# Two small DMAs through DRAM in place of a diagonal product: spreading the token factors of the norms in a two-layer hybrid decoder trunk

## The chip, the cores and the metric

The kernel runs on one core of one Trainium2 chip. The metric is the device time of one execution in microseconds (us); lower is better. Engines are named as in the profile: PE (TensorE matmul) and PEld (its weight loads), DVE (VectorE), ACT (ScalarE), POOL (GpSimd) and SP (SyncE, which here only issues DMAs). A time such as "at 298.30" counts from the first instruction of the profiled execution.

## The reference, cut to what matters

```python
def rmsnorm(x, g):
    y = x * rsqrt(mean(x * x, axis=-1) + EPS)        # one factor r per token
    return y * g                                     # one gain per channel

for l in range(2):                                   # x is (256 tokens, 1024)
    h = rmsnorm(x, norm1[l])
    hq, hf, hi, hg, aq, ak, av, ga, gb = split_cols(h @ w_in[l])
    ...                                              # gated recurrence, windowed attention
    x = x + mix @ w_o[l]
    h2 = rmsnorm(x, norm2[l])
    x = x + (silu(h2 @ w_gate[l]) * (h2 @ w_up[l])) @ w_down[l]
return rmsnorm(x, final_norm)
```

All is float32. The norm's factor r belongs to a token, so it may be left out of the matmul's input and multiplied into its result.

## The kernel before, in words

Every weight comes from DRAM as a 1 MB tile `raw` (SP's queue), and is split into a high part `wh` (ACT, a cast) and a low part `wl` (DVE, `raw - wh`); three matmuls of the parts make one product of nearly full precision. Five `wh` and `wl` tiles rotate. The 256 tokens are two blocks `t` of 128.

A `Norm` object holds what one norm needs. `turn` transposes x on PE, multiplies by the gain and splits it into `xx`, the input of the matmuls, *without* the token factor. `square`, `partial` and `scale` sum the squares; the last step is a power on POOL, which leaves the factor of each token in `r[t]`, a column of 128 partitions by 1.

Where a product has the tokens on its partitions (`form_a`: attention's inputs, values, gates), the factor is `r[t]` itself, the scale operand of the instruction that empties PSUM. Where it has the tokens along the row (`form_b`: the recurrence's f and q, called `pb` in the trace, and the FFN's gate `pg` and up `pu`), each partition needs the factors of all 256 tokens. `spread` (L321) makes that tile, `rb`, 128 partitions by 256. Before the change it takes, for each t, a DVE multiply of the identity by `r[t]` (tile `dg`, one buffer) and a float32 matmul of an all-ones matrix with `dg` into the PSUM tile `rp` (tag "at", two buffers, shared with attention); then an ACT copy takes `rp` to `rb` (one buffer). The profile counts each of these matmuls as two, since float32 goes through PE in two passes.

`spread` is called four times, once for each of the two norms in each layer:

- norm1 (`n1`): at L715, ahead of the second half of the values `v`. The first reader of `rb` is the multiply of f at L726, behind two `pb` blocks.
- norm2 (`n2`): at L835, within the first `gate_up` (L817), as soon as the first gate block is out of PSUM. The first reader is `mid` (L824): DVE multiplies `zg` by `rb`, ACT takes the sigmoid, DVE multiplies the two. Up blocks `pu` are emptied (`join`, L259) behind that.

Work is issued engine by engine in one order that a scheduler sets from the order of the code: every engine runs its own list from the front, so an instruction that waits holds all behind it. In `gate_up` DVE's list has, behind the multiply by `rb`, the splits `wl` of the next weights and the joins that give PSUM buffers back to PE. There are four PSUM buffers for matmul blocks (tag "mm"); a `gate_up` uses all four (two `pg`, two `pu`), so the next `gate_up`'s first `pu` needs the join of this one's first `pu`. Recorded lines of compute instructions are all L55, the helper that records them, so the trace is read by tiles.

Of the kernel before, what the change touches and what calls it, by code (L numbers as in the profile page):

```python
# [7 lines left out]
F32 = mybir.dt.float32  # L8
# [4 lines left out]
ALU = mybir.AluOpType  # L13
AX = mybir.AxisListType

P = 128
D = 1024
S = 256
NT = S // P
# [21 lines left out]
def trunk(ctx, tc, x, norm1, w_in, lb_logits, hg_norm, attn_sinks, w_pa, w_pb, w_o, norm2,  # L41
          w_gate, w_up, w_down, final_norm, const_f, out):
    nc = tc.nc
    pinned, pe_order = [False], [False]

    class Ordered:
        def __init__(self, engine):
            self.engine = engine
            self.always = engine is nc.tensor
# [10 lines left out]
    V, A, G, T = (Ordered(e) for e in (nc.vector, nc.scalar, nc.gpsimd, nc.tensor))  # L60
# [7 lines left out]
    wp = ctx.enter_context(tc.tile_pool(name="wp", bufs=NW))  # L68
    big = ctx.enter_context(tc.tile_pool(name="big", bufs=6))
    sm = ctx.enter_context(tc.tile_pool(name="sm", bufs=2))  # L70
    pp = ctx.enter_context(tc.tile_pool(name="pp", bufs=2, space=bass.MemoryType.PSUM))

    def psum(name, tag="mm"):
        return pp.tile([P, 512], F32, tag=tag, name=name, bufs=4 if tag == "mm" else 2)
# [13 lines left out]
    ones = cp.tile([P, P], F32, tag="ones", name="ones")  # L88
    G.memset(ones, 1.0)
    ident = cp.tile([P, P], F32, tag="ident", name="ident")  # L90
# [185 lines left out]
    class Norm:  # L276
        def __init__(self, gain, name):
            self.gain, self.name = gain, name
            self.xx = hp.tile([P, KT, 2, S], F32R, tag="xx", name=f"xx_{name}")
            self.xh, self.xl = self.xx[:, :, 0, :], self.xx[:, :, 1, :]  # L280
            self.rb = sm.tile([P, 1, S], F32, tag="rb", name=f"rb_{name}", bufs=1)
            self.ss = sm.tile([P, NT, 3], F32, tag="ss", name=f"ss_{name}")
            self.r = [sm.tile([P, 1], F32, tag=f"r{t}", name=f"r_{name}{t}") for t in range(NT)]

# [34 lines left out]
            yield 1  # L319

        def spread(self):  # L321
            rp = psum(f"rp_{self.name}", "at")
            for t in range(NT):
                dg = sm.tile([P, P], F32, tag="dg", name=f"dg_{self.name}{t}", bufs=1)
                tc.keep_in_program_order(V.tensor_scalar(dg, ident, self.r[t], None, ALU.mult))
                T.matmul(rp[:, t * P:(t + 1) * P], ones, dg, start=True, stop=True)
            A.copy(self.rb[:, 0, :], rp[:, :S])

        def wide(self):
            return self.rb.to_broadcast([P, 2, S])  # L330
# [32 lines left out]
    def layer(l, n1):  # L363
# [349 lines left out]
        for c in range(2):  # L713
            if c == 1:
                spread()  # L715
            yield from proj(f"v{c}", lambda t, ps: evac_scaled(v[t][:, c * 512:(c + 1) * 512], ps, rs[t]))
# [293 lines left out]
```

## Time and profile before

| | us |
|---|---|
| median of three runs | 951.02 (951.01 to 951.48) |
| the profiled execution | 951.18 |
| its span, first to last instruction | 949.5 |
| PE busy | 934.3 |
| DVE busy | 678.5 |
| ACT busy | 538.4 |
| POOL busy | 16.5 |

The mean granted clock of PE is 0.998. DMA moves 161.11 MB in 110930 packets, 170 GB/s on average, nearly all of it the weights on SP's queue; ACT issues a few small loads at the start and half of the output. POOL issues no DMA. The time outside the span (951.18 less 949.5) is 1.7 us.

How to read the rows of the timeline: start, duration, engine, line, operation, tiles as out<-in, sizes, how many were merged into the row, and in brackets how long the engine was idle ahead of it and what ended that. Matmuls overlap in the pipe, so the distance from one start to the next is what a matmul costs PE, not its duration.

### The profile page before, as it was taken

To read this page: it belongs to the slowest core of one execution; us is meant where nothing else is said; L and a number is where in the kernel's file an instruction comes from. 1 tells how busy PE (TensorE), PEld (TensorE's weight loads), DVE (VectorE), ACT (ScalarE), POOL (GpSimd) and SP (SyncE) were. 2 spreads that over 40 slices of the span, in tenths; PEclk is the share of its full clock that TensorE was granted. 3 is DMA by queue.
4 is the path that set the end of the run, shared out by engine and by line. 5 is a ranking of instruction groups with operands and counts; after the bars stand their busy time and mean duration, and the time that the engine had idled before them with its cause. 6 is when DMAs were issued, how large, how long until landed. Compare 5 with 4: busy or idle time off the path is not lost.

```text
span 949.5 us, 14350 instructions
## 1 busy us (share of the span) xinstructions
PE 934.3 (98%) x5706; PEld 778.0 (82%) x5706; DVE 678.5 (71%) x1176; ACT 538.4 (57%) x914; POOL 16.5 (2%) x28
## 2 busy tenths in 40 slices
PE   7999999999999999999999999999999999999996
PEld 5878887888888888888878888878788888888885
DVE  6567879976677766766575677898857777667664
ACT  6556596545446545554465776955454565455542
POOL 1000000000000000000000000000000000000000
PEclk9999999999999999999999999999999999999999
DMA  7645454544455566556466444554445566556541
GB/s 282 225 128 175 143 167 137 168 143 159 154 176 177 180 193 203 179 181 198 153 203 197 133 134 133 177 179 134 151 154 185 160 203 191 177 181 202 193 134 44
DMA packets 110930, 161.11 MB, mean 170 GB/s; under 512 B 2768, under 2 KB 64400, under 8 KB 110864
## 3 DMA queue, kind: packets, MB, share of 16 engines
q1 hardware_dynamic: 110160, 159.12, 51.6%
q10 hardware_dynamic: 704, 1.10, 0.3%
q8 instruction: 44, 0.72, 0.3%
q14 instruction: 22, 0.18, 0.1%
HBM read 159.15 MB, written 1.05 MB: 169 GB/s over the span
## 4 chain that ended last, share of the span: by engine, by line
PE 95%; DVE 2%; ACT 2%; DMA 0%; issue 0%; POOL 0%; POOLq 0%; ACTq 0%; SPq 0%
PE pg L55 13%; PE pu L55 13%; PE acc L55 12%; PE pb L55 9%; PE yb L55 5%; PE ga L55 5%; PE gb L55 5%; PE gate L55 5%; PE wo L55 5%; PE ya L55 5%; PE aq L55 5%; PE v L55 4%; PE akv L55 2%; PE qk L55 1%; PE o L55 1%; PE pv L55 1%
## 5 line engine op out<-in xcount | busy, mean ns | idle before, releaser
L55 DVE TENSOR_TENSOR wl<-raw,wh 128x1024 fp32r<-128x1024 f32 x300 | 365.7, 1222 | 146.4 <-ACT wh L55 144.5
L55 ACT CAST wh<-raw 128x1024 fp32r<-128x1024 f32 x300 | 315.0, 1052 | 203.7 <-PE acc L55 61.3
L55 PE MATMUL pu<-xx_n,wh 128*128 128x512 f32 x352 | 125.1, 398 | 0.0
L55 PE MATMUL pg<-xx_n,wh 128*128 128x512 f32 x352 | 125.0, 398 | 0.0
L55 PE MATMUL pu<-xx_n,wl 128*128 128x256 f32 x352 | 91.8, 281 | 0.0
L55 PE MATMUL pg<-xx_n,wl 128*128 128x256 f32 x352 | 91.6, 281 | 0.0
L55 PE MATMUL pb<-xx_n,wh 128*128 128x512 f32 x256 | 91.3, 403 | 0.0
L55 PEld LDWEIGHTS pg<-xx_n,wh 128*128 128x128 f32 x352 | 64.8, 188 | 12.4
L55 PEld LDWEIGHTS pu<-xx_n,wh 128*128 128x128 f32 x352 | 64.8, 188 | 11.9
L55 PEld LDWEIGHTS pu<-xx_n,wl 128*128 128x128 f32 x352 | 66.5, 189 | 4.0
L55 PEld LDWEIGHTS pg<-xx_n,wl 128*128 128x128 f32 x352 | 66.5, 189 | 4.0
L55 PE MATMUL acc<-wl,ah 128*128 128x512 f32 x176 | 69.0, 392 | 0.0
L55 PE MATMUL acc<-wh,al 128*128 128x512 f32 x176 | 68.8, 391 | 0.0
L55 PE MATMUL acc<-wh,ah 128*128 128x512 f32 x176 | 68.2, 391 | 0.0
L55 PE MATMUL pb<-xx_n,wl 128*128 128x256 f32 x256 | 66.9, 281 | 0.0
L55 PEld LDWEIGHTS pb<-xx_n,wh 128*128 128x128 f32 x256 | 46.6, 188 | 11.3 <-issue 2.4
L55 PEld LDWEIGHTS pb<-xx_n,wl 128*128 128x128 f32 x256 | 48.2, 189 | 2.4
L55 ACT COPY zg<-pg 128x256 f32<-128x256 f32 x44 | 16.4, 373 | 57.2 <-PE pg L55 57.2
L55 PE MATMUL ga<-wh,xx_n 128*128 128x512 f32 x128 | 43.6, 402 | 0.0
L55 PE MATMUL gb<-wh,xx_n 128*128 128x512 f32 x128 | 43.1, 400 | 0.0
L55 PE MATMUL v<-wh,xx_n 128*128 128x512 f32 x128 | 41.2, 394 | 0.0
L55 PE MATMUL gate<-wh,xx_n 128*128 128x512 f32 x128 | 40.9, 393 | 0.0
(221 smaller groups left out, 1667.8 us busy)
## 6 DMA issues: line engine op xcount, KB each, us to landing
raw<-in_w_in SPq DMA_DIRECT2D x58, 1024.0 KB, 5.1
raw<-in_w_gate SPq DMA_DIRECT2D x22, 1024.0 KB, 5.1
raw<-in_w_up SPq DMA_DIRECT2D x22, 1024.0 KB, 5.1
raw<-in_w_down SPq DMA_DIRECT2D x22, 1024.0 KB, 5.0
raw<-in_w_pb SPq DMA_DIRECT2D x8, 1024.0 KB, 5.0
raw<-in_w_pa SPq DMA_DIRECT2D x8, 1024.0 KB, 5.0
raw<-in_w_o SPq DMA_DIRECT2D x8, 1024.0 KB, 5.0
raw<-in_w_in SPq DMA_DIRECT2D x4, 512.0 KB, 6.2
```

The lines of the kernel that those rows point to most:

```text
L55: ins = call(*args, **kw)
```

## The change

`spread` no longer computes. It issues, on POOL's queue, one DMA for each t that writes the 128 factors of `r[t]` (one 4-byte value from each partition) to a row of a small DRAM tile `row` (2 by 128), and one DMA that reads `row` back as 256 values to each of 128 partitions, which is `rb`. The tile `dg`, the PSUM tile `rp`, eight DVE multiplies, eight matmul calls and four ACT copies go; twelve DMA issues on POOL come. All else in the code stays.

```diff
+    dp = ctx.enter_context(tc.tile_pool(name="dp", bufs=1, space=bass.MemoryType.DRAM))
...
             self.rb = sm.tile([P, 1, S], F32, tag="rb", name=f"rb_{name}", bufs=1)
+            self.row = dp.tile([NT, P], F32, tag=f"row_{name}", name=f"row_{name}")
...
         def spread(self):
-            rp = psum(f"rp_{self.name}", "at")
-            for t in range(NT):
-                dg = sm.tile([P, P], F32, tag="dg", name=f"dg_{self.name}{t}", bufs=1)
-                tc.keep_in_program_order(V.tensor_scalar(dg, ident, self.r[t], None, ALU.mult))
-                T.matmul(rp[:, t * P:(t + 1) * P], ones, dg, start=True, stop=True)
-            A.copy(self.rb[:, 0, :], rp[:, :S])
+            for t in range(NT):
+                nc.gpsimd.dma_start(self.row[t].rearrange("(p o) -> p o", o=1), self.r[t])
+            nc.gpsimd.dma_start(self.rb[:, 0, :], self.row.rearrange("t p -> (t p)").partition_broadcast(P))
```

The lists of instructions move in three places that matter below. A name's last number is that of its buffer.

On POOL, norm2 of layer 0 was two powers and nothing more:

```order
L55 TENSOR_TENSOR r_n_00_2615<-r_n_00_2615,mhalf 128x1
L55 TENSOR_TENSOR r_n_01_2616<-r_n_01_2616,mhalf 128x1
L55 TENSOR_TENSOR r_n_10_4268<-r_n_10_4268,mhalf 128x1
L55 TENSOR_TENSOR r_n_11_4269<-r_n_11_4269,mhalf 128x1
L55 TENSOR_TENSOR oss_6077<-oss_6077,mhalf 128x4
```

It is now this, with each write issued right behind its power, and the read of `row` behind a wait for both writes to have landed:

```order
L55 TENSOR_TENSOR r_n_00_2614<-r_n_00_2614,mhalf 128x1
L325 DMA row_n_0_2612<-r_n_00_2614 128x1
L55 TENSOR_TENSOR r_n_01_2615<-r_n_01_2615,mhalf 128x1
L325 DMA row_n_0_2612<-r_n_01_2615 128x1
L326 DMA rb_n_0_2611<-row_n_0_2612 128x256
```

So the DMAs are issued where r becomes ready, not where the code calls `spread`; for norm1 that is far ahead of the call.

On DVE, the same norm's first `gate_up` before, from the first `dg` to the first multiply by `rb` and the joins of `pu` behind it:

```order
L55 TENSOR_SCALAR dg_n_00_2872<-ident,r_n_00_2615 128x128
L55 TENSOR_TENSOR wl_2909<-raw_2783,wh_2908 128x1024
L55 TENSOR_SCALAR dg_n_01_2875<-ident,r_n_01_2616 128x128
L55 TENSOR_TENSOR wl_2931<-raw_2805,wh_2930 128x1024
L55 TENSOR_TENSOR zg_2835<-pg_2832,zg_2835 128x256
L55 TENSOR_TENSOR zg_2835<-zg_2835,rb_n_0_2613 128x512
L55 TENSOR_TENSOR wl_2937<-raw_2805,wh_2936 128x1024
L55 TENSOR_TENSOR zg_2835<-zg_2835,sgm_2836 128x512
L55 TENSOR_TENSOR wl_2968<-raw_2906,wh_2967 128x1024
L55 TENSOR_TENSOR sgm_2836<-pu_2833,sgm_2836 128x256
```

And after:

```order
L55 TENSOR_TENSOR wl_2903<-raw_2782,wh_2902 128x1024
L55 TENSOR_TENSOR wl_2925<-raw_2804,wh_2924 128x1024
L55 TENSOR_TENSOR zg_2834<-pg_2831,zg_2834 128x256
L55 TENSOR_TENSOR zg_2834<-zg_2834,rb_n_0_2611 128x512
L55 TENSOR_TENSOR wl_2931<-raw_2804,wh_2930 128x1024
L55 TENSOR_TENSOR zg_2834<-zg_2834,sgm_2835 128x512
L55 TENSOR_TENSOR wl_2962<-raw_2900,wh_2961 128x1024
L55 TENSOR_TENSOR sgm_2835<-pu_2832,sgm_2835 128x256
```

Only the two `dg` are gone; the multiply by `rb` stands in the same place and now waits for a DMA.

On PE, the end of the values in layer 1 and attention's scores `qk` behind it, before:

```order
L55 MATMUL v_1_4841<-wh_4782,xx_n_1_4265 128x512
L55 MATMUL rp_n_1_4832<-dg_n_11_4836,ones 128x128
L55 MATMUL qk_4911<-kT_4428,qT_4431 128x128 x2
L55 MATMUL qk_4921<-kT_4428,qT_4431 128x256
L55 MATMUL qk_4912<-kT_4428,qT_4431 128x128 x2
L55 MATMUL qk_4922<-kT_4428,qT_4431 128x256
L55 MATMUL qk_4921<-kT_4428,qT_4431 128x256
L55 MATMUL qk_4922<-kT_4428,qT_4431 128x256
L55 MATMUL pb_4956<-xx_n_1_4265,wh_4854 128x512
```

And after:

```order
L55 MATMUL v_1_4831<-wh_4777,xx_n_1_4259 128x512
L55 MATMUL qk_4901<-kT_4423,qT_4426 128x128
L55 MATMUL qk_4902<-kT_4423,qT_4426 128x128
L55 MATMUL qk_4901<-kT_4423,qT_4426 128x128
L55 MATMUL qk_4902<-kT_4423,qT_4426 128x128
L55 MATMUL qk_4911<-kT_4423,qT_4426 128x256
L55 MATMUL qk_4912<-kT_4423,qT_4426 128x256
L55 MATMUL qk_4911<-kT_4423,qT_4426 128x256
L55 MATMUL qk_4912<-kT_4423,qT_4426 128x256
L55 MATMUL pb_4946<-xx_n_1_4259,wh_4844 128x512
```

The product `rp` is gone, and the scores now alternate between the two halves of the partitions (tiles 4901 and 4902, 4911 and 4912), as they do in layer 0 in both kernels. Otherwise PE's list is the old one without its eight `rp`, but for a `pb` matmul of layer 1 that now stands ahead of a `qp` block, and SP's list is the same.

## Prediction

> **What bounds the kernel now.** I read the page first, then PE's own waits, then the timeline around each of the four places where the factors are spread.
>
> ```profile
> span 949.5 us, 14350 instructions
> PE 934.3 (98%) x5706; PEld 778.0 (82%) x5706; DVE 678.5 (71%) x1176; ACT 538.4 (57%) x914; POOL 16.5 (2%) x28
> PE 95%; DVE 2%; ACT 2%; DMA 0%; issue 0%; POOL 0%; POOLq 0%; ACTq 0%; SPq 0%
> ...
> PE rp_n L55 <- DVE dg_n L55: 0.7, 1, 0.7
> ...
> PE qp L55 <- DVE att0l L55: 0.3, 1, 0.3
> ```
>
> PE is busy for 98% of the span and makes 95% of the chain that ended last. So a matmul removed from PE is time won, unless something else becomes late; work removed from DVE and ACT is worth nothing by itself. After its start PE waits for DVE in only two places: once for `dg`, which the change removes, and once, in layer 0, for attention (`qp`), which may take back what was won ahead of it.
>
> **What goes.** The rows of the three operations, all four calls together:
>
> ```profile
> L55 PE MATMUL rp_n<-dg_n,ones x16: 270/274/377, 68.5 to 766.0; 128*128 128x128 f32 x16
> L55 DVE TENSOR_SCALAR dg_n<-ident,r_n x8: 276/282/291, 68.2 to 765.4; 128x128 f32<-128x128 f32 x8
> L55 ACT COPY rb_n<-rp_n x4: 362/372/373, 70.4 to 766.3; 128x256 f32<-128x256 f32 x4
> ```
>
> DVE loses 8 x 0.28 = 2.3 us and ACT 4 x 0.37 = 1.5 us, both beside PE's work: counted as nothing. PE's price is the shift of the matmuls behind `rp`. In norm2 of layer 0 (PE only, weight loads and other engines left out between):
>
> ```profile
> 298.30 0.38 PE L55 MATMUL rp_n<-dg_n,ones 128*128 128x128 f32 x2
> 298.44 0.48 PE L55 MATMUL pg<-xx_n,wh 128*128 128x512 f32 x1
> 298.75 0.28 PE L55 MATMUL pg<-xx_n,wl 128*128 128x256 f32 x1
> 298.87 0.39 PE L55 MATMUL pg<-xx_n,wh 128*128 128x512 f32 x1
> 299.10 0.28 PE L55 MATMUL pg<-xx_n,wl 128*128 128x256 f32 x1
> ...
> 299.93 0.48 PE L55 MATMUL rp_n<-dg_n,ones 128*128 128x128 f32 x2
> 300.16 0.36 PE L55 MATMUL pu<-xx_n,wl 128*128 128x256 f32 x1
> 300.37 0.40 PE L55 MATMUL pu<-xx_n,wh 128*128 128x512 f32 x1
> ```
>
> From wh to wl is normally 0.23 (298.87 to 299.10), behind `rp` 0.31; with the 0.14 that `rp` itself holds PE, the first costs 0.22. The second holds 0.23 and stretches wl to wh from 0.12 (298.75 to 298.87) to 0.21: 0.32. Norm2 gives 0.54 in layer 0, and I take the same in layer 1.
>
> Norm1 of layer 0, where PE also waits for `dg`, with the DVE rows behind it and the later wait of `qp`:
>
> ```profile
> 67.24 0.61 PE L55 MATMUL v<-wh,xx_n 128*128 128x512 f32 x2
> 68.50 0.49 PE L55 MATMUL rp_n<-dg_n,ones 128*128 128x128 f32 x2 [0.65 <-DVE dg_n L55]
> 68.75 0.48 PE L55 MATMUL v<-wl,xx_n 128*128 128x512 f32 x1
> ...
> 69.69 2.36 DVE L55 TENSOR_TENSOR wl<-raw,wh 128x1024 fp32r<-128x1024 f32 x2
> ...
> 72.43 0.29 DVE L55 CUSTOM_DVE_ANT_0 sp<-qk,cf 128x128 f32<-128x128 f32 x1 [0.38 <-PE qk L55]
> ...
> 87.64 1.10 PE L55 MATMUL qp<-ident,aq 128*128 128x128 f32 x8 [0.27 <-DVE att0l L55]
> ```
>
> Without `rp`, v's next matmul would start two normal steps (0.23 each) behind 67.24, at 67.70, not 68.75: 1.05. With 0.3 for the second `rp`, PE comes 1.35 earlier to `qk`. DVE can't follow all the way: its two `wl` end at 72.05, and without two `dg`, which each hold it about 0.2, at 71.65; so it takes up `qk` at 71.65, not 72.43, 0.8 earlier, and passes that on through attention to `att0l`. At 87.64 PE waits for just that. Of 1.35 I keep 0.8; between 0 and 1.35 it can't be known better.
>
> Norm1 of layer 1: two `rp` at 0.22, and the order of `qk` behind them:
>
> ```profile
> 71.68 1.58 PE L55 MATMUL qk<-kT,qT 64*128 64x128 f32 x16
> ...
> 537.04 2.46 PE L55 MATMUL qk<-kT,qT 64*128 64x128 f32 x16
> ```
>
> The same sixteen matmuls of 64 rows take 1.58 in layer 0, where they alternate between the two halves of the partitions, and 2.46 in layer 1, where the scheduler put them in runs of one half, the second half behind the copy that frees `rp`'s buffer. After the change layer 1 has the alternating order: 0.88 less. In all 1.32 at PE; DVE wins less (its 0.4 from `dg`), so some will be given back as in layer 0. I keep 1.0.
>
> The sum: 0.8 + 0.54 + 1.0 + 0.54 = 2.9 us. Everything kept it is 1.35 + 0.54 + 1.32 + 0.54 = 3.75; with norm1's gain all given back, 1.1.
>
> **What comes.** POOL issues three DMAs for each norm; nobody else is queued on POOL near them. For norm1 they start when r is ready, before `dg` read it (68.2); the first reader is here:
>
> ```profile
> 83.97 0.68 DVE L55 TENSOR_TENSOR f<-f,rb_n 128x512 f32<-128x512 f32 x1
> ```
>
> That is over 15 us of cover, hidden; layer 1 has the like. If it were gone, DVE would wait, with weight splits and attention behind it.
>
> Norm2 is tight. The last factor is ready, the multiply wants `rb`, and the rows that follow it to PE's next need, the first `pu` of the second `gate_up`:
>
> ```profile
> 294.11 0.56 POOL L55 TENSOR_TENSOR r_n<-r_n,mhalf 128x1 f32<-128x1 f32 x1 [4.39 <-DVE r_n L55]
> ...
> 301.44 0.69 DVE L55 TENSOR_TENSOR zg<-zg,rb_n 128x512 f32<-128x512 f32 x1
> ...
> 303.05 1.05 ACT L55 CAST wh<-raw 128x1024 fp32r<-128x1024 f32 x1 [0.26 <-PE pu L55]
> ...
> 304.13 1.22 DVE L55 TENSOR_TENSOR wl<-raw,wh 128x1024 fp32r<-128x1024 f32 x1 [0.27 <-ACT wh L55]
> 305.28 0.75 DVE L55 TENSOR_TENSOR sgm<-pu,sgm 128x256 f32<-128x256 f32 x2
> ...
> 308.44 0.40 PE L55 MATMUL pu<-xx_n,wh 128*128 128x512 f32 x1
> ```
>
> Factors are in SBUF at 294.67. Behind the multiply stand a `wl`, the second `zg` multiply, a `wl`, and the join that frees the PSUM buffer of the first `pu`; it ends at 305.65 (half of 0.75 behind 305.28), 4.2 behind the multiply, or 3.95 if late, since ACT's idle 0.26 goes. PE wants the buffer at 308.44, 0.54 earlier after the change: 307.9. So the multiply may start as late as 303.95, and the two DMAs in a row have 303.95 - 294.67 = 9.2 us, rounded down, before PE loses anything. Beyond that every us costs PE a us, in each layer. The first `wl` that the wait holds is needed only by the fourth block of the second `gate_up`, later than that.
>
> On POOL the write of the first factor now stands ahead of the power of the second; POOL idled 4.39 us there, so an issue shorter than that costs nothing, and a longer one delays the second factor by the rest. The bytes are nothing beside the weights: four reads of 128 KB add 0.5 MB to 161, and I charge the loads nothing for them.
>
> No row shows a DMA issued by POOL. The nearest, median us from issue to landing, and one issue on ACT's queue:
>
> ```profile
> rows<-in_norm ACTq DMA_DIRECT2D x2, 8.0 KB, 3.2
> rows<-in_lb_logits ACTq DMA_DIRECT2D x1, 8.0 KB, 5.1
> nsink<-in_attn_sinks ACTq DMA_DIRECT2D x1, 16.0 KB, 6.2
> gfin<-in_final_norm ACTq DMA_DIRECT2D x1, 512.0 KB, 3.7
> out<-x SPq DMA_DIRECT2D x2, 256.0 KB, 2.1
> ...
> 2.69 0.44 ACTq L180 DMA_DIRECT2D nsink<-in_attn_sinks  x1
> ```
>
> The least is a store at 2.1 and a broadcast at 3.7 (`gfin`): 5.8. The most is 5.1 and 6.2 (`nsink`, a broadcast among the start's loads) and 0.44 for each issue: 12.2. I take 3.2 for the write, since weights load beside it, and 3.7 for the broadcast, which like `gfin` goes to 128 partitions from a row, and 0.44 twice: 7.8. `rb` lands at 302.5; DVE waits about 1.5 us and PE not at all.
>
> [...]
>
> **The rivals.** *Late factors, slower.* If both DMAs take what the loaded ones took, 12.2, PE is held 12.2 - 9.2 = 3.0 in each layer: 951.0 - 2.9 + 6.0 = 954.1. It decides from 10.65 us (break-even, 9.2 + 2.9/2), and is slower by over 1.9 us from 11.6. For it: the DMA engines are full with weights just then, and 128 pieces of 4 bytes are nothing like these rows. Against it: the rows at 5.1 and 6.2 queue behind one another at the program's start. 0.11.
>
> *POOL's issue held by DVE.* Should DVE's long two-input instructions (`wl`, 1.22) hold POOL from SBUF, each of two issues could wait out one: 7.8 + 2.4 = 10.2, 1.0 late in each layer, 951.0 - 2.9 + 2.0 = 950.1. Against it, POOL's power beside a `wl` in this norm:
>
> ```profile
> 289.15 0.56 POOL L55 TENSOR_TENSOR r_n<-r_n,mhalf 128x1 f32<-128x1 f32 x1 [48.15 <-DVE r_n L55]
> ...
> 289.26 2.36 DVE L55 TENSOR_TENSOR wl<-raw,wh 128x1024 fp32r<-128x1024 f32 x2 [0.19 <-ACT wh L55]
> ```
>
> It took 0.56 beside a `wl`, no more than at 294.11, and two `wl` took 2.36, their usual 1.2 each. [...] 0.11.
>
> *PE's gain in norm1 swallowed.* If DVE's and ACT's attention work sets the pace in both layers, only norm2's 1.1 is left: 949.9. For it: PE's wait at `qp`; against it: that wait is 0.27 long, the only one. 0.12.
>
> **How the numbers follow.** The profiled execution would go from 951.18 to 948.3; the runs' median lies 0.16 lower, so 948.1. That is 0.31% less; 0.2% is 1.9 us, about what a measurement can tell from no change. My forecast has 0.66 (faster), the two middle rivals 0.23 (within 0.2%), late factors 0.11 (slower). The range: down to 951.0 - 3.75 and 0.45, the spread of the runs, 946.8; up over both middle cases, and up to the break-even of lateness, 951.0.
>
> **What would show it.** Right: PE's waits have no `rp`; `qk` of layer 1 takes about 1.6; the first `zg` multiply waits 0 to 2 us for a DMA and PE's `pu` behind it for nothing; `qp`'s wait in layer 0 grows to about 0.8. Wrong: PE waiting for DVE `sgm` at the second `gate_up`, POOL's issues of over 1 us, or `rb` landing over 9.2 us after the power.

## The result, and the profile after

The changed kernel takes 967.45 us (median of five runs, 966.36 to 969.05) against 951.02 for the kernel before (median of five, 950.77 to 951.48): 1.0172 of its time, interval 1.0161 to 1.0183. It is slower by 16.4 us, where 948.1 was forecast. Its profiled execution takes 967.84 us.

The page after: the span, the busy times, and the shares of the chain that ended last.

```profile
span 966.1 us, 14327 instructions
PE 934.3 (97%) x5690; PEld 778.0 (81%) x5690; DVE 675.4 (70%) x1168; ACT 535.6 (55%) x910; POOL 23.7 (2%) x40
PE 89%; DMA 4%; DVE 3%; ACT 2%; issue 1%; POOL 0%; POOLq 0%; SPq 0%; DVEq 0%; ACTq 0%
```

PE's busy time is as before, 934.3, and its instructions are fewer by the sixteen `rp`, but its part of the chain fell from 95% to 89%, and DMA, which had 0%, has 4%. PE's waits (total, times, longest):

```profile
PE pu L55 <- DVE sgm L55: 16.8, 2, 9.0
...
PE qp L55 <- DVE att0l L55: 0.6, 1, 0.6
```

The wait for `dg` is gone and `qp`'s has doubled, as forecast. New is the one that the prediction named as the sign of its being wrong: two waits, one in each layer, at the first `pu` of the second `gate_up`. The chain of layer 0's norm2 (start, duration, what) says why:

```profile
293.03 0.57 POOL r_n L55
293.60 0.28 issue
293.89 12.87 DMA row_n<-r_n
306.76 0.02 issue
306.78 0.04 POOLq L326
306.82 0.50 issue
307.32 3.34 DMA rb_n<-row_n
...
310.76 0.69 DVE zg L55
...
314.24 0.43 DVE sgm L55
...
314.71 7.37 PE pu L55 x32
```

From the power's end at 293.60 to `rb` at 310.66 it is 17.1 us, of which the second write alone is 12.87. The DMA issues (KB each, median us from issue to landing) show that it was no accident of one place:

```profile
rb_n<-row_n POOLq DMA_DIRECT2D x4, 128.0 KB, 4.6
row_n<-r_n POOLq DMA_DIRECT2D x8, 0.5 KB, 10.8
```

The wait is not all of the loss. PE's rows around it, and the granted clock (the column ahead of the last two) in stretches of 3 us:

```profile
306.55 0.39 PE L55 MATMUL pg<-xx_n,wh 128*128 128x512 f32 x1
314.71 0.80 PE L55 MATMUL pu<-xx_n,wh 128*128 128x512 f32 x1 [7.77 <-DVE sgm L55]
315.31 0.41 PE L55 MATMUL pu<-xx_n,wl 128*128 128x256 f32 x1
315.52 0.63 PE L55 MATMUL pu<-xx_n,wh 128*128 128x512 f32 x1
...
316.16 0.63 PE L55 MATMUL pu<-xx_n,wh 128*128 128x512 f32 x1
```

```profile
306.00:309.00 3.00, 0.94 (x6) 0.57 (x4) 0.00 (x0) 0.00 (x0) 0.55 (x1) 1.00 0.59 156
309.00:312.00 3.00, 0.00 (x0) 0.00 (x0) 1.24 (x2) 0.52 (x1) 0.00 (x0) 0.86 0.33 81
312.00:315.00 3.00, 0.29 (x1) 0.29 (x2) 2.99 (x5) 2.83 (x6) 0.00 (x0) 0.50 0.33 80
315.00:318.00 3.00, 3.00 (x10) 2.52 (x11) 2.98 (x5) 1.92 (x4) 0.00 (x0) 0.50 0.79 275
```

Behind the wait PE is granted half its clock (0.50). A pair of `pu` matmuls then starts every 0.64 (315.52 to 316.16) instead of every 0.35, until about 318.

To place every microsecond I compared the start of each PE matmul with its counterpart in the trace before (by position, `rp` left out). Negative means earlier than before:

| step | changed kernel |
|---|---|
| norm1, layer 0, at `qk` | -1.41 |
| given back at `qp` | +0.36 |
| norm2, layer 0 | -0.58 |
| wait and slow clock, layer 0 | +9.52 |
| norm1, layer 1 | -1.34 |
| norm2, layer 1 | -0.59 |
| wait and slow clock, layer 1 | +10.58 |
| all the rest | +0.10 |
| last matmul | +16.64 |

The gains are 3.6 and the two stalls 20.1. These steps serve as a yardstick for the experiments.

### The profile page after: what moved, and what is told of

Read it like the earlier page. It is cut to its first block, busy times and chain, and to the rows that moved or that the text cites. A ratio compares the mean times of both kernels' runs of the same rounds, so it can differ in the third digit from the quotient of the medians.

```text
span 966.1 us, 14327 instructions
## 1 busy us (share of the span) xinstructions
PE 934.3 (97%) x5690; PEld 778.0 (81%) x5690; DVE 675.4 (70%) x1168; ACT 535.6 (55%) x910; POOL 23.7 (2%) x40
## 3 DMA queue, kind: packets, MB, share of 16 engines
HBM read 159.68 MB, written 1.05 MB: 166 GB/s over the span
## 4 chain that ended last, share of the span: by engine, by line
PE 89%; DMA 4%; DVE 3%; ACT 2%; issue 1%; POOL 0%; POOLq 0%; SPq 0%; DVEq 0%; ACTq 0%
PE pu L55 12%; PE acc L55 12%; PE pg L55 11%; PE pb L55 8%; PE yb L55 5%; PE ga L55 5%; PE gb L55 5%; PE gate L55 5%; PE ya L55 5%; PE aq L55 5%; PE v L55 4%; PE wo L55 4%; DMA row_n<-r_n 3%; PE akv L55 2%; DVE wl L55 2%
## 5 line engine op out<-in xcount | busy, mean ns | idle before, releaser
L55 PE MATMUL pu<-xx_n,wh 128*128 128x512 f32 x352 | 128.0, 405 | 16.8 <-DVE sgm L55 16.8
L55 ACT COPY zg<-pg 128x256 f32<-128x256 f32 x44 | 16.4, 373 | 51.9 <-PE pg L55 51.9
```

The source lines that it names most:

```text
L55: ins = call(*args, **kw)
```

## The experiments

The theory was now: the gains are real, norm1's DMAs are hidden, and all of the loss is norm2's late factor, through PE's wait and the slower clock behind it. Rivals were that the small DMAs hurt by themselves, that POOL's queue is slow, and that the packets queue behind the weights.

**n1_only and n2_only: each half of the change alone.**

```diff
         def spread(self):
+            (self.spread_dma if self.name.startswith("n1") else self.spread_dg)()
```

`spread_dg` is the old body of `spread`, `spread_dma` the new one; n2_only has `"n2"` in that line.

> The norms ahead of the mixers (norm1) spread by the DMAs, the norms ahead of the FFNs (norm2) by the diagonal product as before. Theory (the whole loss is PE waiting behind the late factors of norm2; norm1's DMAs are hidden): norm1's gains alone remain, 1.1 in layer 0 and 1.0 in layer 1, so 951.0 - 2.1 = 948.9, and PE waits for no DMA. Rival (twelve small DMAs hurt by themselves, through the weight loads or POOL's queue): no gain, 951 or more. Rival (norm1's DMAs are late as well): DVE waits for rb ahead of f, 951 to 955.

> Norm2 by the DMAs, norm1 by the diagonal product. Theory (PE waits 7.8 and 9.0 us behind the late rb, and its matmuls run slower for some us behind each wait, 1.5 each, less norm2's gain of 0.55 each): 951.0 + 16.8 + 3.0 - 1.1 = 969.7. Rival (norm1's DMAs share the blame): clearly less, under 965.

Measured: n1_only 948.87, ratio 0.9976 (0.9967 to 0.9985); n2_only 969.14, ratio 1.0192 (1.0178 to 1.0206). Both are the theory's numbers to within 0.6. Half of the change is a gain, though its writes take a median of 9.6 us there too: norm1 has cover for that. The other half is the whole loss.

**no_factor and no_factor_2: the removal without anything in its place.**

```diff
-            self.rb = sm.tile([P, 1, S], F32, tag="rb", name=f"rb_{name}", bufs=1)
+            self.rb = rb_all
...
         def spread(self):
-            for t in range(NT):
...
+            pass
```

> No spreading at all: rb is a constant tile of ones, filled at the start, so the token factor is left out of everything multiplied by rb. It shows what the removal alone is worth, with rb never late and no DMA added. Theory (my steps on the gain side hold): 951.0 - 3.2 = 947.8, by the shifts of PE's matmuls in the changed kernel ahead of its stalls (1.5 in layer 0, 1.65 in layer 1); the prediction's own sum gave 2.9, so 948.1. Rival (later waits swallow it): 949.5 to 951.

> The same question as no_factor, with the tile of ones filled later, so that the loads at the program's start stand in the order of the other kernels (in no_factor the new fill moved one load of ACT's queue ahead of the first weight cast, and PE started 2.1 us later). The token factor is left out of what rb multiplies. PE's, DVE's, ACT's and SP's lists are those of the changed kernel. Theory (the removal is worth 1.05 + 0.57 + 1.3 + 0.57): 951.0 - 3.5 = 947.5. Rival (an empty start only moved the loss): 949 to 951.

The first came out at 949.99, ratio 0.9990 (0.9981 to 0.9998), and says little: its PE was already 2.1 us late at 22 us, before any norm was spread, with the loads on ACT's queue in another order. The second, with the loads in the order of the others, took 947.69, ratio 0.9958 (0.9945 to 0.9970); its steps at PE are -1.41, +0.36, -0.58, -1.34 and -0.57, as in the changed kernel. So the removal is worth about 3.5 us and nothing later swallows it.

**deferred: the same late factors, nothing waiting behind them.**

```diff
                 join(z[:, 1], pg[1])
-                mid()
                 join(sgm[:, 0], pu[0])
...
+                late.append(rest)
+                return
             else:
...
+                if late:
+                    late.pop()()
                 mid()
```

`rest` does what `mid` and the split did, with a tile of its own for the sigmoid; the second `gate_up` calls it behind its gate joins.

> All norms by the DMAs as in the changed kernel, but in the first gate_up the joins of pu no longer stand behind the multiply by rb: the sigmoid goes to a tile of its own, and the multiply is pinned behind the first gate join of the second gate_up, some 5 us later in DVE's list, with nothing behind it that PE needs before 319. Theory (lateness is the only cost): PE waits for nothing there, though rb lands no earlier (16 us behind the power), and the time is that of the kernel without factors, 947.5 to 948.5. Rival (the small DMAs or their packets slow the weight loads): PE still waits, for wl or wh, and the time stays above 951.

Measured: 948.73 (947.75 to 950.11), ratio 0.9978 (0.9969 to 0.9987). In layer 0 PE waits for nothing; in layer 1, where the write took 13.1, DVE's multiply and then PE still wait:

```profile
777.87 0.69 DVE L55 TENSOR_TENSOR zg<-zg,rb_n 128x512 f32<-128x512 f32 x1 [7.39 <-DMA rb_n<-row_n]
...
782.95 0.50 PE L55 MATMUL pu<-xx_n,wh 128*128 128x512 f32 x1 [0.92 <-DVE sgm L55]
```

That costs 1.3 there, about the distance to 947.5. The DMAs themselves, with all their packets, cost nothing that shows.

**delay_12, delay_24, delay_20 and delay_40: lateness without a DMA.** POOL makes norm2's `rb` itself behind a chain of N small operations.

```diff
+            d = sm.tile([P, 1], F32, tag="dly", name=f"dly_{self.name}")
+            src = self.r[1]
+            for _ in range(N):
+                G.tensor_tensor(d, src, mhalf[:, 0:1], ALU.mult)
+                src = d
+            G.tensor_tensor(self.rb[:, 0, :], ones2, d.to_broadcast([P, S]), ALU.mult)
```

> No DMA and no product: for norm2 POOL makes rb itself, out of a chain of 12 small operations behind the second power and one 128x256 operation; norm1's rb is a tile of ones (the factors are left out of what rb multiplies). Lists of the other engines as in the changed kernel. The chain at 0.3 to 0.56 an operation puts rb 5 to 9 us behind the power. Theory (PE has some 9.2 us of cover, and only lateness counts): PE waits for nothing there, 947.5. Rival (the cover is less than I worked out, or POOL's work holds DVE): a wait of PE for sgm, over 949.

> The same with 24 small operations, 9 to 16 us behind the power. Theory: PE waits for sgm by what rb is later than 9.2 us, and then its matmuls run slowly for some us, about 1.5 us in each layer once the wait is several us long, with no DMA in it. Rival (the slow matmuls behind the stall come from the DMAs, not from PE's own pause): the wait alone, no loss behind it.

These two went to 1023.92 and 1032.58 and test nothing: the last operation, a power over 128x256, took 41.1 us on POOL. With a multiply in its place:

> No DMA and no product for norm2: POOL fills rb itself behind a chain of 20 small operations (0.34 us each, as the chain of delay_24 showed) and one 128x256 multiply in place of the power that took 41 us there; norm1's rb is a tile of ones, so token factors are left out of what rb multiplies. rb is ready about 7 + 1 us behind the power. Theory (9.2 us of cover): PE waits for nothing there, 947.7. Rival (less cover than worked out): a wait of PE for sgm, over 949.

> The same with 40 operations: rb ready about 14.5 us behind the power, so 5.3 beyond the cover. Theory: PE waits 5 to 6 us for sgm in each layer and loses a further 1 to 1.5 behind it to a lower granted clock, with no DMA in it: 947.7 + 2 x 6.5 = 960 to 962. Rival (the slow matmuls behind the stall come from the DMAs): the wait alone, 958.

Measured: delay_20 947.40, ratio 0.9957 (0.9943 to 0.9971), PE waits for nothing there; delay_40 961.65 (959.30 to 961.97), ratio 1.0108 (1.0092 to 1.0124). In delay_40 POOL's fill, DVE's multiply, PE's wait, and the granted clock behind it:

```profile
306.38 0.61 POOL L55 TENSOR_TENSOR rb_n<-ones,dly_n 128x256 f32<-128x256 f32 x1
307.02 0.69 DVE L55 TENSOR_TENSOR zg<-zg,rb_n 128x512 f32<-128x512 f32 x1 [7.17 <-POOL rb_n L55]
310.97 0.80 PE L55 MATMUL pu<-xx_n,wh 128*128 128x512 f32 x1 [4.29 <-DVE sgm L55]
```

```profile
309.00:312.00 3.00, 1.03 (x3) 0.93 (x4) 2.96 (x6) 2.18 (x5) 0.00 (x0) 0.76 0.58 161
312.00:315.00 3.00, 3.00 (x13) 2.58 (x13) 2.97 (x5) 1.84 (x3) 0.00 (x0) 0.67 0.64 208
315.00:318.00 3.00, 3.00 (x19) 2.63 (x18) 3.00 (x5) 1.95 (x3) 0.00 (x0) 1.00 0.95 315
```

The multiply could have started at 307.02 - 4.29 = 302.73, and the power ended at 293.33: the cover is 9.4 us. PE came 5.9 us later over this stall (from -1.92 to +3.98), 1.6 more than it waited, with no DMA of POOL's in the kernel. The 0.67 in the second stretch is a mean: in stretches of 1 us the clock is 0.50 from 311 to 314 and 1.00 from 314 on. In delay_20, with the same kind of chain and no pause, it is 1.00 there. So the slow clock comes with PE's own pause, not with the DMAs.

**probe and probe_2: what the write costs by itself.** The kernel before, with one dead DMA behind each `gate_up` in several forms.

> The kernel before plus one dead DMA at the end of each gate_up, from a tile just made, in different forms; read by issue and landing, not by the kernel's time. col: 128 pieces of 4 bytes to one DRAM row, as the change does. few: 16 pieces of 4 bytes. apart: 128 pieces of 4 bytes, each 512 bytes from the next. wide: 128 pieces of 512 bytes. one: 512 bytes from one partition. prow: 128 pieces of 4 bytes to a row in SBUF. act_: the same from ACT's queue. Theory A (many pieces of 4 bytes in DRAM end slowly): col 9 to 16 us, apart and wide much less or few much less, act_col as slow as col. Theory B (POOL's queue is slow whatever it carries): all of POOL's near 10, those of ACT 2 to 4. Theory C (small packets wait behind the weights on the 16 DMA engines): all forms alike on both queues, with a spread that goes with the load.

> The kernel before plus one dead DMA to DRAM from POOL's queue at the end of each gate_up, 128 pieces (then 1 and 4) of 4 bytes at strides of 4, 32, 64, 128 and 256 bytes, and 128 pieces of 16, 32, 64 and 128 bytes side by side. Theory (writes of parts of one DRAM block follow one another): slow, 5 us and more, while several pieces share a block, so at strides below the block's size and for 16 and 32 bytes side by side, and 3 to 4 us from some size on, 64 bytes as a guess; one piece 3. Rival (it is the number of 4-byte pieces): all strides slow alike, and one piece fast.

The median us to landing in probe (the queue is in the second column):

```profile
probe_ac_wide<-zg POOLq DMA_DIRECT2D x1, 64.0 KB, 3.0
...
prow<-zg POOLq DMA_DIRECT2D x3, 0.5 KB, 3.4
...
probe_aa_col<-zg POOLq DMA_DIRECT2D x1, 0.5 KB, 8.5
probe_ab_few<-zg POOLq DMA_DIRECT2D x1, 0.1 KB, 6.2
probe_ad_one<-zg POOLq DMA_DIRECT2D x1, 0.5 KB, 2.8
probe_af_apart<-zg POOLq DMA_DIRECT2D x1, 0.5 KB, 3.0
probe_ag_col<-zg POOLq DMA_DIRECT2D x1, 0.5 KB, 8.1
...
probe_be_col<-zg ACTq DMA_DIRECT2D x1, 0.5 KB, 9.5
```

The change's form takes 7.4 to 9.5 in five tries, on both queues, so POOL's queue is not the cause (theory B falls). The other forms take 1.4 to 6.2, beside the same loads of weights, so not all forms are alike (theory C falls). In probe_2 (names are cut by the trace; in order 4 bytes at a stride of 4, of 32, of 64, and 16 bytes side by side):

```profile
robe_aa_128of4every<-zg POOLq DMA_DIRECT2D x1, 0.5 KB, 8.0
robe_ab_128of4every<-zg POOLq DMA_DIRECT2D x1, 0.5 KB, 6.3
obe_ac_128of16every<-zg POOLq DMA_DIRECT2D x1, 2.0 KB, 3.8
robe_ad_128of4every<-zg POOLq DMA_DIRECT2D x1, 0.5 KB, 2.9
...
robe_bh_128of4every<-zg POOLq DMA_DIRECT2D x1, 0.5 KB, 8.1
robe_bi_128of4every<-zg POOLq DMA_DIRECT2D x1, 0.5 KB, 3.0
```

The last two are strides of 4 and of 32 once more: 8.1 and 3.0. The packet records of POOL's queue divide each time into two parts, up to the last packet and from there to the landing:

| write | issue to last packet | last packet to landing |
|---|---|---|
| 4 bytes side by side in DRAM, probes (5) | 1.4 to 2.5 | 5.7 to 7.0 |
| 4 bytes at strides of 32 to 512 bytes (11) | 1.3 to 5.3 | 0.4 to 1.0 |
| 16, 32, 64, 128, 512 bytes side by side (11) | 1.5 to 3.6 | 0.3 to 1.3 |
| 16 pieces of 4 bytes side by side (3) | 4.7 to 5.5 | 0.3 to 0.9 |
| 128 pieces of 4 bytes to a row in SBUF (3) | 2.3 to 4.6 | 0.6 to 0.8 |

Only the change's form has the long second part; 128 pieces of 4 bytes are not slow as such, a stride of 32 is enough. From POOL's queue `few`, one of the two tries at a stride of 32 (6.3) and one of the three `apart` (5.6) were late in their first part; why was not tried. One piece of 4 bytes took 2.8 and 3.6, four side by side 3.1 and 4.3. Neither of my expectations was quite right: no block of 64 bytes shows, and 16 bytes side by side are quick (3.8 and 3.0).

**row_in_sbuf: the row in SBUF instead of DRAM, all else as changed.**

```diff
-            self.row = dp.tile([NT, P], F32, tag=f"row_{name}", name=f"row_{name}")
+            self.row = sm.tile([1, NT, P], F32, tag="row", name=f"row_{name}", bufs=1)
```

> The changed kernel with one difference: row lies in SBUF, as 256 values on one partition, and not in DRAM; the two writes and the broadcast stay DMAs on POOL's queue, and the lists of PE, DVE, ACT and SP stay the same. Theory (128 pieces of 4 bytes that lie side by side in DRAM end slowly, 7.4 to 9.5 us in the probe, in SBUF 2.9 to 5.3): the last write takes 3 to 6, the broadcast 3 to 5, the issues 1.1, so rb lands 7 to 12 us behind the power, PE waits 0 to 3 us in each layer, and the time is 947.6 to 951. Rival (waiting behind the weights' packets is the larger part): the write still takes 9 or more, 955 to 967.

Measured: 948.44, ratio 0.9968 (0.9956 to 0.9981), with the same lists on every engine but POOL. POOL's rows in layer 0's norm2, and DVE's first multiply:

```profile
293.94 0.58 POOL L325 DMA_DIRECT2D row_n<-r_n  x1 [0.29 <-POOL r_n L55]
296.55 0.55 POOL L326 DMA_DIRECT2D rb_n<-row_n  x1 [2.02 <-DMA row_n<-r_n]
```

```profile
303.08 0.69 DVE L55 TENSOR_TENSOR zg<-zg,rb_n 128x512 f32<-128x512 f32 x1 [2.94 <-DMA rb_n<-row_n]
```

The write lands 2.0 us behind its issue, while the DMA engines move 223 GB/s, nearly all of it weights; in the changed kernel they moved 78 GB/s over the write's 12.9. The broadcast takes 6.4, more than the 3 to 5 expected, the multiply starts at 303.08, 9.4 behind the power's end at 293.65, just past the edge of the cover, and PE loses 0.3 in each layer. So waiting behind the weights was not the larger part of the write's time.

**one_dram and sbuf_halves.** In one_dram only the second token block goes through DRAM; in sbuf_halves both go through the row in SBUF, each with a broadcast of its own.

```diff
             for t in range(NT):
...
+                sl = slice(t * P, (t + 1) * P)
+                nc.gpsimd.dma_start(self.row[0:1, t, :], self.r[t])
+                nc.gpsimd.dma_start(self.rb[:, 0, sl], self.row[0:1, t:t + 1, :].to_broadcast([1, P, P]))
```

These lines are those of sbuf_halves. In one_dram the second pass writes to a DRAM row, `drow`, and reads from it.

> The changed kernel, but the first token block's factors go through a row in SBUF with a broadcast of their own, and only the second block's through DRAM, with its own broadcast of 128 values. Theory (in the changed kernel the second write's packets start only when the first write to DRAM has landed): the second write now takes what it takes alone, 7.4 to 9.5 us, not 12.9 and 14.2; rb lands 12 to 14 us behind the power, PE waits 3 to 5 us in each layer, with 1.6 behind each: 957 to 961. Rival (its packets wait behind the weights): the write still takes 12 to 14 there, 964 to 967.

> The row in SBUF as in row_in_sbuf, and a broadcast for each token block by itself, so that the second one brings 128 values to each partition and the first one is out of the way. Theory (the broadcast's 6.4 us came from its size): the second takes 3 to 5, rb is whole 7 to 8 us behind the power, PE waits for nothing there: 947.4 to 947.9, 0.5 to 1 less than row_in_sbuf. Rival (the broadcast from one partition costs the same whatever its size): 6 us again, and no gain over row_in_sbuf.

one_dram took 963.92, ratio 1.0132 (1.0117 to 1.0148); the chain in layer 0:

```profile
294.82 7.32 DMA drow_n<-r_n
...
302.43 4.97 DMA rb_n<-drow_n
```

The second write takes 7.3 here and 7.9 in layer 1, not 12.9 and 14.2: the rest of the changed kernel's write came with the first write to DRAM ahead of it. The packet records fit: in the changed kernel all but one of the 16 packets with the second write's data in layer 0's norm2 come from 299.35 on, just as the first write has landed at 299.45. In one_dram `rb` lands 12.9 and 14.4 us behind the power. The time is 3 above the expected range, because the broadcast took 5.0 and 5.9 and POOL's second power came 0.9 later behind the first broadcast's issue.

sbuf_halves took 947.93, ratio 0.9961 (0.9949 to 0.9974). Its DMA issues:

```profile
rb_n<-row_n POOLq DMA_DIRECT2D x8, 64.0 KB, 4.1
row_n<-r_n POOLq DMA_DIRECT2D x8, 0.5 KB, 4.0
```

PE waits for nothing behind `rb`, and the time is within 0.3 of no_factor_2. This version has the whole gain, 0.39%.

## Why the prediction was wrong, point by point

- *What bounds the kernel.* Right: PE's list sets the end, and what PE was spared came out at the end wherever nothing was late.
- *What goes.* Right, and a little low. Norm1 of layer 0: 1.41 at `qk` and 1.05 kept (said 1.35 and 0.8); norm2 0.58 and 0.59 (said 0.54 each); norm1 of layer 1: 1.34, 1.28 kept (said 1.32 and 1.0), with `qk` at 1.58 in the alternating order, as forecast. The sum is 3.5, not 2.9.

```profile
544.44 1.58 PE L55 MATMUL qk<-kT,qT 64*128 64x128 f32 x16
...
86.57 1.09 PE L55 MATMUL qp<-ident,aq 128*128 128x128 f32 x8 [0.63 <-DVE att0l L55]
```

- *Norm1's DMAs hidden.* Right, by n1_only; in layer 0 `rb` landed at 42.28 in the changed kernel, 22.1 behind the second write's issue at 20.23, and its first reader comes at about 83.
- *The cover of 9.2 us.* Right: 9.4 by delay_40, and 9.1 by row_in_sbuf, which loses 0.3 at 9.4.
- *The two DMAs take 7.8.* **This step failed.** It took 3.2 for the write, from a load of 16 rows at the program's start, and the write took 12.87 and 14.22. The issues (0.85 in all against 0.88) were sized well. The broadcast (3.34 and 3.19 against 3.7) came out so partly by luck: it ran while PE, DVE and ACT stood still; in deferred, where they went on and the DMA engines moved 262 and 317 GB/s instead of 190 and 67, the same broadcast took 5.8 and 6.5. The text itself said that 128 pieces of 4 bytes are nothing like its rows, and then let those rows set the upper end, 12.2. Even with 7.3 for the write, as alone, the two DMAs would have taken 7.3 + 3.3 + 0.9 = 11.5, already beyond the break-even (one_dram, with that write and a slower broadcast, took 12.9). The other 5.5 and more is a second cause that no term of the sum had: another write to DRAM issued 5 us ahead.
- *Beyond the cover every us costs PE a us.* Too little. 7.77 of waiting cost 9.5, and 4.29 cost 5.9, since PE comes back at half the granted clock: behind 4.3 us of pause (delay_40) and behind 7.8 (the changed kernel) it was 0.50 for the first 3.0 and 3.3 us of PE's work. Behind the 0.92 of deferred a pair of `pu` starts every 0.36 (783.41 to 783.77), as without a pause. The 3.0 us that *Late factors* held PE lie between, and no run here has a pause between 0.9 and 4.3 us at that place, so whether 954.1 was too low for its own case stays open.
- *The rivals.* *Late factors, slower* is what happened, with its mechanism and place, at 0.11, but not with its size: it had 12.2 us for the DMAs and 954.1, against 17.1 and 967.45. *POOL's issue held by DVE* did not: issues took 0.55 to 0.75. *PE's gain swallowed* did not: 0.36 of 1.41.
- *What a write takes at the least.* The least row of the sum was a store at 2.1; the second writes of row_in_sbuf took 1.9 to 2.0 in all four norms. From POOL's queue the probes show 0.3 to 1.3 us from the last packet to the landing for the other forms to DRAM, and 5.7 to 7.0 for this one.

## What to carry to other kernels

A transfer's price belongs to its form, not to its bytes (512 bytes took 1.4 to 9.5 us in probe and probe_2): where the trace has no row of the same number and size of pieces, the same layout at the target and the same queue, the upper end must be open, and a step whose cover is only 1.4 us longer than its estimate is a coin toss. When a column of single values has to become a row, let the DMA write it to SBUF and start the broadcast of each part as soon as that part is there (947.93 against 967.45). Price a pause of PE of 4 to 9 us at its length and 1.6 to 2.5 us more, as the eight of 4.3 to 9.0 us here cost.

## What the runs showed of the hardware

- In the probes a DMA of 128 pieces of 4 bytes, one from each partition, side by side into one DRAM row landed 5.7 to 7.0 us behind its last packet from POOL's queue, and was as slow from ACT's (5.3 and 6.8 behind the last packet, 8.3 and 9.5 in all); at strides of 32 bytes and more, or into SBUF, it was 0.4 to 1.0. From POOL's queue the data went in 16 packets of 32 bytes, so 8 pieces to a packet; from ACT's in 128 packets of 4. Sixteen pieces side by side did not have the long wait (0.3 to 0.9). The mechanism is open.
- A second such write, issued 3.7 to 5.6 us behind the first, landed 7.3 to 10.2 behind it in three of four places of the changed kernel. In norm2 most of its packets came only when the first had landed, in norm1 of layer 0 more than 2 us after that. In norm1 of layer 1 it landed only 2.3 behind, and 2.1 in n1_only and in deferred. That is the place with the shortest distance between the two issues, 3.7 us against 5.0 to 5.6. Whether this makes the difference, and whether it is their common queue or their neighbouring rows that hold the second write, was not tried.
- The broadcast of 256 values from one partition of SBUF took 6.4 to 6.6, that of 128 values 3.9 to 4.2; from DRAM 256 values took 3.2 to 7.4, and 128 values 5.0 to 6.8; what sets that was not tried.
- Behind eight pauses of PE of 4.3 to 9.0 us (the changed kernel, n2_only, one_dram, delay_40) PE worked at a granted clock of 0.50 for 3.0 to 5.0 us, and came 1.6 to 2.5 us later than the wait alone explains.
- A power over 128x256 took POOL 41.1 us, a multiply of the same shape 0.61.
